# The normaliser of the decode states goes by transfer into and out of the states' 129th column

## The chip, the cores and the metric

The kernel runs on one core of a Trainium2 chip. The metric is the device time of one launch in microseconds (us); the figure compared is the median of several runs. A core has TensorE (matrix products; "PE" in the profile, "PEld" for its weight loads), VectorE ("DVE"), ScalarE ("ACT"), GpSimd ("POOL") and SyncE ("SP", which here issues all transfers). Each of them works through its own list of instructions in a fixed order, so an instruction that waits holds everything behind it in its list. Transfers run on 16 DMA engines.

## The reference

One decoder layer on 1024 prompt tokens and on 8 decode sequences of 8 tokens each. Half of the mixing heads are retention heads, half are mLSTM heads (4 of each, 128 wide). Cut to the mLSTM part that the change touches:

```python
def step(carry, inp):
    C, n, m = carry                       # matrix memory, normaliser, stabiliser
    ...
    num = (einsum('bhts,bhsv->bhtv', s, vc)
           + inter[..., None] * einsum('bhvd,bhtd->bhtv', C, qc))
    den_dot = sum(s, axis=-1) + inter * einsum('bhd,bhtd->bht', n, qc)
    ...
    C_new = decay[..., None, None] * C + einsum('bhsv,bhsd->bhvd', vc * wl[..., None], kc)
    n_new = decay[..., None] * n + einsum('bhs,bhsd->bhd', wl, kc)
```

`n` (128 numbers for each head and sequence) is treated like one more column of `C`: the same product with q and the same update. For the 8 decode sequences `C` and `n` come from the inputs and go back to the outputs.

## The kernel before, in words

The work is staged: input projections with the 8 heads between them, output projection, up-projection with a convolution, down-projection. `mix_head(hd, ml)` does one head, first the 4 retention heads, then the 4 mLSTM heads m0 to m3.

In one mLSTM head `proj` makes q, k and v, each from one 128x1024 weight tile that is fetched by `stage_w` (line 133, tile `st_in`, 2 buffers) and split by ScalarE (L145, `wh_in`) and VectorE (L147, `wl_in`) into a high and a low part for the matmuls of lines 159 to 161. Then `front` prepares two chunks of 128 tokens, `pair_of` does two chunks, `sample` does the 64 decode tokens, and `finish` normalises; the decode tokens stand third in `order = [[0, 1], [2, 3], [8], [4, 5], [6, 7]]`.

The decode states of a head lie in the tile `sb` of 128 partitions x 8 sequences x 129 columns: 128 columns for `C`, the 129th for `n`. There is one buffer for it (`bufs=1`), shared by all heads, so the next head's states can be written into it only when this head's are stored. Its steps: line 511 fetches `C` into the first 128 columns; lines 512 to 515 fetch `n` into a tile `sn` of its own and copy it on VectorE into the 129th column; line 617 multiplies `sb` with the queries on TensorE; lines 626 and 634 update it on VectorE; line 637 stores `C` (`out_cs`); lines 639 and 640 copy the 129th column back to `sn` and store that (`out_ns`).

Beside the mLSTM heads runs `weight_sums` (lines 692 to 707), which needs nothing from them: 40 times it fetches a 128x1024 group of up-projection weights into one of two tiles `sg` (lines 699 and 700, one buffer each), makes four differences on GpSimd (L704) and stores them to a DRAM scratch `sd` (L705). A fetch into a tile waits until the store before it has left that tile. All of these transfers and all others stand in the one list of SyncE.

The order in each list is not the order of the text: a scheduler puts the instructions in order at build time by its own estimate of the times, and inserts the waits on semaphores. What stands where is shown below with the change.

Of the kernel before, what the change touches and what calls it, by code (L numbers as in the profile page):

```python
# [10 lines left out]
F32 = mybir.dt.float32  # L11
# [5 lines left out]
P = 128  # L17
# [3 lines left out]
NB = 8  # L21
# [71 lines left out]
def hybrid_layer_kernel(ctx: ExitStack, tc: tile.TileContext, a: dict, o: dict):  # L93
    nc = tc.nc
# [32 lines left out]
    def bank(p, cols, name, rows=P, dt=F32):  # L127
        t = p.tile([P, 512], dt, tag="bank", name=name)
        return t[:rows, :cols]
# [95 lines left out]
    m2 = mpool("m2", bufs=2)  # L225
# [251 lines left out]
    def mix_head(hd, ml):  # L477

        nm = ("m" if ml else "r") + str(hd)
# [30 lines left out]
        sb = m2.tile([P, NB, 129], F32, tag="sb", bufs=1, name=f"sb_{nm}")  # L510
        nc.sync.dma_start(sb[:, :, :P], a["sc" if ml else "sr"][hd].rearrange("p (s v) -> p s v", s=NB))
        if ml:
            sn = m2.tile([P, NB], F32, tag="sn", name=f"sn_{nm}")
            nc.sync.dma_start(sn, a["sn"][hd])
            nc.vector.tensor_copy(sb[:, :, P], sn)
        dec = m2.tile([P, 16], F32, tag="dec", name=f"dec_{nm}")

        def front(cs):
# [52 lines left out]
        def stats(on, po, i0, L, n, mv, name):  # L571
            nc.scalar.activation(on[:n, i0:i0 + L, :W], po, AF.Copy)
            for i in range(i0, i0 + L):
                st = m2.tile([P, 6], F32, tag="bn", name=f"bn_{name}{i}")
                nc.vector.bn_stats(st[:n], on[:n, i, :P])
                nc.vector.bn_aggr(mv[:n, i, :], st[:n])

        def finish(on, mv, c0, L, name):

            n = rows_of(c0)  # L580
            sh = [n, L]
            small = lambda tag: m2.tile([P, 4], F32, tag=tag, name=f"{tag}_{name}")[:n, :L]
            vv, A = small("vv"), small("A")
            if ml:
                den, rd = small("den"), small("rd")
                dd = on[:n, :L, P]
                nc.vector.scalar_tensor_tensor(den, dd, -1.0, dd, ALU.mult, ALU.max)
                nc.vector.tensor_tensor(den, den, cols[:n, c0:c0 + L, hd], ALU.max)
                nc.vector.reciprocal(rd, den)
                nc.vector.tensor_tensor(vv, mv[:n, :L, 1], rd, ALU.mult)  # L590
                nc.vector.tensor_tensor(vv, vv, rd, ALU.mult)
            else:
                xs_ = lambda t: cst[:n, t + 9 * hd + c0:t + 9 * hd + c0 + L]
                rd = xs_(C_XI)
                nc.vector.tensor_tensor(vv, mv[:n, :L, 1], xs_(C_XI2), ALU.mult)
            nc.vector.tensor_scalar(vv, vv, EPS, None, ALU.add)
            rstd_small(A, vv, m2, name, sh)
            nc.vector.tensor_tensor(A, A, rd, ALU.mult)
            ps = bank(psB, L * n, f"yt_{name}")
            for i in range(L):  # L600
                nc.vector.tensor_scalar(on[:n, i, :P], on[:n, i, :P], mv[:n, i, 0:1], A[:, i:i + 1],
                                        ALU.subtract, ALU.mult)
                nc.tensor.transpose(ps[:, i * n:(i + 1) * n], on[:n, i, :P], ident[:n, :n])
            y = yT[hid // 2][:, hid % 2, c0 * CH:c0 * CH + L * n]
            gain = vec[:, V_HEAD + hid:V_HEAD + hid + 1]
            if hid in EARLY:
                nc.vector.scalar_tensor_tensor(y, ps, gain, y, ALU.mult, ALU.mult)
            else:
                nc.scalar.activation(y, ps, AF.Copy, scale=gain)

        def sample(kz, vt, qs, pt):
            qv = qs[:, 0, :TS] if ml else q[:, LP:]
            nc.vector.tensor_copy(qown, qv.rearrange("p (s l) -> p s l", s=NB))
            po = bank(psB, W, f"o_{nm}8", rows=TS)
            nc.tensor.matmul(po, pt[:TS, 0, :TS], vt[:TS, 0, :W], start=True, stop=False)
            for i in range(NB):
                nc.tensor.matmul(po, qx[:, i * TS:(i + 1) * TS], sb[:, i, :W], start=False, stop=i == NB - 1)
            on = m2.tile([P, 4, 129], F32, tag="on", bufs=3, name=f"on_{nm}s")
            mv = m2.tile([P, 4, 2], F32, tag="mv", bufs=3, name=f"mv_{nm}s")
            stats(on, po.unsqueeze(1), 0, 1, TS, mv, f"{nm}s")  # L620
            vx = m2.tile([TS, NB, 129], F32, tag="vx", bufs=1, name=f"vx_{nm}")[:, :, :W]
            e = nc.vector if ml else nc.gpsimd
            e.tensor_tensor(vx, vt[:TS, 0, :W].unsqueeze(1).broadcast_to([TS, NB, W]),  # L623
                            cst[:TS, C_BLK:C_BLK + NB].unsqueeze(2).broadcast_to([TS, NB, W]), ALU.mult)
            if ml:
                e.tensor_tensor(sb, sb, dec[:, 8:16].unsqueeze(2).broadcast_to([P, NB, W]), ALU.mult)
            step = 3 if ml else 4
            for j in range(0, NB, step):
                m = min(step, NB - j)
                up = bank(psB, m * W, f"us_{nm}{j}").rearrange("p (s v) -> p s v", s=m)  # L630
                nc.tensor.matmul(up, kz[:TS, 0, :], vx[:, j:j + m, :], start=True, stop=True)
                sj = sb[:, j:j + m, :W]
                if ml:
                    nc.vector.tensor_tensor(sj, sj, up, ALU.add)
                else:
                    nc.vector.scalar_tensor_tensor(sj, sj, math.exp(LS * LG[hd]), up, ALU.mult, ALU.add)
            nc.sync.dma_start(o["cs" if ml else "ss"][hd].rearrange("p (s v) -> p s v", s=NB), sb[:, :, :P])
            if ml:
                nc.vector.tensor_copy(sn, sb[:, :, P])
                nc.sync.dma_start(o["ns"][hd], sn)  # L640
            return lambda: finish(on, mv, 8, 1, f"{nm}s")

        S = None
# [35 lines left out]
        for i, cs in enumerate(order):  # L679
            cur, ready = ready, front(order[i + 1]) if i + 1 < len(order) else None  # L680
            done = sample(*cur) if cs == [8] else pair_of(cs[0], *cur)
            if todo:
                todo()
            todo = done
            next(rows, None)
# [24 lines left out]
    for hd in range(NH):  # L710
        mix_head(hd, False)
        if hd == 0:
            gate_proj()
            rows = gate_rows()
# [3 lines left out]
    for hd in range(NH):  # L718
        mix_head(hd, True)
# [610 lines left out]
```

## Time and profile before

| | us |
|---|---|
| median of 3 runs | 1426.72 |
| the runs | 1421.37 to 1428.78 |
| the profiled execution | 1421.1 |
| its span | 1419.3 |
| TensorE busy | 1350.3 (95%) |
| VectorE busy | 1005.3 (71%) |
| ScalarE busy | 587.7 (41%) |
| GpSimd busy | 386.3 (27%) |
| the 16 DMA engines busy, mean | 40% |

The span is the profiled execution on the core; the 1.8 us between it and the execution's own time lie around it. Times in rows of the profile count from the start of the span. A row of a timeline has the start, the duration, the engine, the line of the kernel, the operation and its tiles ("out<-in"), and in brackets the idle time before it and what ended that. "SPq" rows are instructions of SyncE that issue a transfer.

### The profile page before, as it was taken

To read this page: it belongs to the slowest core of one execution; us is meant where nothing else is said; L and a number is where in the kernel's file an instruction comes from. 1 tells how busy PE (TensorE), PEld (TensorE's weight loads), DVE (VectorE), ACT (ScalarE), POOL (GpSimd) and SP (SyncE) were. 2 spreads that over 40 slices of the span, in tenths; PEclk is the share of its full clock that TensorE was granted. 3 is DMA by queue.
4 is the path that set the end of the run, shared out by engine and by line. 5 is a ranking of instruction groups with operands and counts; after the bars stand their busy time and mean duration, and the time that the engine had idled before them with its cause. 6 is when DMAs were issued, how large, how long until landed. Compare 5 with 4: busy or idle time off the path is not lost.

```text
span 1419.3 us, 26935 instructions
## 1 busy us (share of the span) xinstructions
PE 1350.3 (95%) x10545; PEld 1324.8 (93%) x10545; DVE 1005.3 (71%) x2030; ACT 587.7 (41%) x1102; POOL 386.3 (27%) x486
## 2 busy tenths in 40 slices
PE   7999899999697799999999999999999999999996
PEld 7899899989687799999999999999999999999995
DVE  7846974464353546656889987877877889896677
ACT  6424543312131223544546444433443445454553
POOL 5200000244454450000244322122222115782000
PEclk9999999999899999999999999999999999999998
DMA  6112111455657652332314343344343358633363
GB/s 234 60 45 78 48 54 56 134 180 193 209 179 225 205 183 75 113 114 73 123 42 145 149 153 125 118 138 145 138 137 130 117 161 308 197 115 99 96 213 126
DMA packets 116286, 192.80 MB, mean 136 GB/s; under 512 B 9024, under 2 KB 74688, under 8 KB 115648
## 3 DMA queue, kind: packets, MB, share of 16 engines
q1 hardware_dynamic: 116160, 191.09, 40.1%
q8 instruction: 83, 1.36, 0.4%
q14 instruction: 43, 0.35, 0.1%
HBM read 134.58 MB, written 56.47 MB: 135 GB/s over the span
## 4 chain that ended last, share of the span: by engine, by line
PE 73%; DMA 13%; DVE 6%; POOL 3%; issue 2%; ACT 2%; SPq 1%; DVEq 0%; POOLq 0%; ACTq 0%
DMA sd<-sg 6%; PE up_S L958 6%; PE up_S L957 6%; PE up_S L956 6%; PE in L161 6%; PE in L159 5%; PE in L160 5%; DMA sg<-in_wu 5%; PE dn L1155 5%; PE dn L1153 5%; PE dn L1154 5%; PE up_A L957 4%; PE up_A L956 4%; PE up_A L958 4%; POOL sg L704 3%
## 5 line engine op out<-in xcount | busy, mean ns | idle before, releaser
L159 PE MATMUL in<-hh,wh_in 128*128 128x272 f32 x1024 | 304.9, 298 | 8.6 <-ACT hh L199 6.7
L161 PE MATMUL in<-hh,wl_in 128*128 128x272 f32 x1024 | 302.2, 296 | 1.4 <-DVE wl_in L147 1.4
L160 PE MATMUL in<-hl,wh_in 128*128 128x272 f32 x1024 | 301.0, 294 | 1.3 <-DVE hl L200 1.3
L159 PEld LDWEIGHTS in<-hh,wh_in 128*128 128x128 f32 x1024 | 196.9, 192 | 10.7 <-ACT hh L199 6.6
L160 PEld LDWEIGHTS in<-hl,wh_in 128*128 128x128 f32 x1024 | 196.3, 192 | 3.8 <-issue 2.1
L161 PEld LDWEIGHTS in<-hh,wl_in 128*128 128x128 f32 x1024 | 196.2, 192 | 3.0 <-DVE wl_in L147 1.9
L704 POOL TENSOR_TENSOR sg<-sg 128x256 f32<-128x256 f32 x160 | 124.4, 790 | 175.5 <-DMA sg<-in_wu 167.8
L145 ACT ACTIVATE wh_up<-st_up 128x1024 fp32r<-128x1024 f32 x84 | 80.5, 959 | 165.4 <-PE up_S L957 99.6
L1082 DVE TENSOR_TENSOR rb<-rb 128x544 fp32r<-128x544 f32 x78 | 76.5, 986 | 37.8 <-ACT rb L1081 37.6
L147 DVE TENSOR_TENSOR wl_up<-st_up,wh_up 128x1024 fp32r<-128x1024 f32 x84 | 95.9, 1142 | 7.9 <-ACT wh_up L145 7.8
L930 DVE TENSOR_TENSOR Uv<-Uv,up_S 128x272 f32<-128x272 f32 (+1 forms) x200 | 66.7, 377 | 46.0 <-PE up_S L958 46.0
L986 POOL TENSOR_TENSOR act<-act 128x544 f32<-128x544 f32 x44 | 70.6, 1604 | 78.3 <-DMA bd<-act 50.0
L1081 ACT ACTIVATE rb<-rb 128x544 fp32r<-128x544 f32 x78 | 50.5, 650 | 75.4 <-DMA rb<-bd 62.8
L1102 POOL TENSOR_TENSOR wd<-wd 128x512 f32<-128x512 f32 x44 | 73.7, 1701 | 27.8 <-DMA wd<-in_wd 15.0
L971 DVE SCALAR_TENSOR_TENSOR c<-Uv,vec,c 128x1024 f32<-128x1024 f32 (+1 forms) x88 | 70.1, 799 | 8.9 <-ACT c L969 8.9
L971 DVE SCALAR_TENSOR_TENSOR c<-Ug,vec,c 128x1024 f32<-128x1024 f32 x88 | 68.6, 819 | 1.3 <-ACT c L969 1.3
L145 ACT ACTIVATE wh_in<-st_in 128x1024 fp32r<-128x1024 f32 x32 | 33.9, 1058 | 54.5 <-PE in L160 48.6
L969 ACT ACTIVATE c<-Ug,vec 128x1024 f32<-128x1024 f32 (+1 forms) x44 | 34.6, 835 | 52.2 <-DVE Ug L934 47.0
L921 POOL MEMSET Ug<- 128x2 f32 x22 | 2.2, 99 | 177.4 <-DVE xr L824 83.7
L147 DVE TENSOR_TENSOR wl_in<-st_in,wh_in 128x1024 fp32r<-128x1024 f32 x32 | 41.1, 1283 | 10.9 <-ACT wh_in L145 10.4
L623 POOL TENSOR_TENSOR vx_r<-vts,cst 64x1024 f32<-64x1024 f32 x4 | 8.3, 2082 | 142.7 <-ACT vts L536 142.7
L958 PE MATMUL up_S<-T1h,wl_up 128*128 128x272 f32 x160 | 46.6, 291 | 0.0
(540 smaller groups left out, 4583.3 us busy)
## 6 DMA issues: line engine op xcount, KB each, us to landing
rb<-bd SPq DMA_DIRECT2D x76, 272.0 KB, 2.9
sg<-in_wu SPq DMA_DIRECT2D x80, 256.0 KB, 3.9
sd<-sg SPq DMA_DIRECT2D x40, 512.0 KB, 4.0
st_up<-sd SPq DMA_DIRECT2D x40, 512.0 KB, 3.7
bd<-act SPq DMA_DIRECT2D x33, 544.0 KB, 4.5
st_in<-in_wi SPq DMA_DIRECT2D x32, 512.0 KB, 4.3
st_up<-in_wu SPq DMA_DIRECT2D x24, 512.0 KB, 4.1
wd<-in_wd SPq DMA_DIRECT2D x44, 256.0 KB, 4.6
```

What stands on the lines that cost most here:

```text
L145: nc.scalar.activation(hi, x, AF.Copy)
L147: eng.tensor_tensor(lo, x, hi.bitcast(F32), ALU.subtract)
L159: nc.tensor.matmul(ps, hi[:, ws], xh, start=k == 0, stop=False)
L160: nc.tensor.matmul(ps, hi[:, ws], xl, start=False, stop=False)
L161: nc.tensor.matmul(ps, lo[:, ws], xh, start=False, stop=k == KT - 1)
L704: nc.gpsimd.tensor_tensor(o_, x, y, op)
L956: nc.tensor.matmul(ps, wh[:, c], xh[:, k, n], start=k == 0, stop=False)
L957: nc.tensor.matmul(ps, wh[:, c], xl[:, k, n], start=False, stop=False)
L958: nc.tensor.matmul(ps, wl[:, c], xh[:, k, n], start=False, stop=k == 3)
L971: nc.vector.scalar_tensor_tensor(c, u(i), cw(i), c, ALU.mult, ALU.add)
L1082: nc.vector.tensor_tensor(lo, x, hi.bitcast(F32), ALU.subtract)
L1102: nc.gpsimd.tensor_tensor(quad(p, out), quad(p, x), quad(p, y), op)
```

## The change

The tile `sn` and its two copies on VectorE go. `n` is fetched by a transfer straight into the 129th column of `sb`, and stored straight from there. `C` and its two transfers stay.

```diff
         sb = m2.tile([P, NB, 129], F32, tag="sb", bufs=1, name=f"sb_{nm}")
         nc.sync.dma_start(sb[:, :, :P], a["sc" if ml else "sr"][hd].rearrange("p (s v) -> p s v", s=NB))
         if ml:
-            sn = m2.tile([P, NB], F32, tag="sn", name=f"sn_{nm}")
-            nc.sync.dma_start(sn, a["sn"][hd])
-            nc.vector.tensor_copy(sb[:, :, P], sn)
+            nc.sync.dma_start(sb[:, :, P], a["sn"][hd])
...
             nc.sync.dma_start(o["cs" if ml else "ss"][hd].rearrange("p (s v) -> p s v", s=NB), sb[:, :, :P])
             if ml:
-                nc.vector.tensor_copy(sn, sb[:, :, P])
-                nc.sync.dma_start(o["ns"][hd], sn)
+                nc.sync.dma_start(o["ns"][hd], sb[:, :, P])
```

The 8 numbers of `n` in a partition lie 129 columns apart in `sb`, so each of the two transfers now moves 1024 pieces of 4 bytes, where it moved 128 pieces of 32 bytes.

The lists of ScalarE and GpSimd keep their order. On VectorE the 8 copies are left out, and in each mLSTM head the decode tokens' last normalising step (`on_m0s`) changes places with the step after it (`kz_m`); TensorE takes three transposes and one matmul in another order there. Two places matter below.

On VectorE, at the end of head m0 (names with `m0s` are its decode tokens), before the change, the copy into the next head's `sb` stands between two small steps of m0's normalising:

```order
L591 TENSOR_TENSOR vv_m0s<-vv_m0s,rd_m0s 64x1
L596 TENSOR_SCALAR vv_m0s<-vv_m0s 64x1
L171 SCALAR_TENSOR_TENSOR t_m0s<-t_m0s,vv_m0s 64x1
L515 COPY sb_m_4493<-sn_m_4495 128x8
L172 SCALAR_TENSOR_TENSOR A_m0s<-t_m0s,r_m0s 64x1
L598 TENSOR_TENSOR A_m0s<-A_m0s,rd_m0s 64x1
L601 TENSOR_SCALAR on_m0s<-on_m0s,mv_m0s,A_m0s 64x128
```

The same place after the change (lines below the edit are numbered 2 or 3 lower):

```order
L589 TENSOR_TENSOR vv_m0s<-vv_m0s,rd_m0s 64x1
L594 TENSOR_SCALAR vv_m0s<-vv_m0s 64x1
L171 SCALAR_TENSOR_TENSOR t_m0s<-t_m0s,vv_m0s 64x1
L172 SCALAR_TENSOR_TENSOR A_m0s<-t_m0s,r_m0s 64x1
L596 TENSOR_TENSOR A_m0s<-A_m0s,rd_m0s 64x1
L526 TENSOR_TENSOR kz_m_4012<-x_m_4007,cols 128x256
L599 TENSOR_SCALAR on_m0s<-on_m0s,mv_m0s,A_m0s 64x128
```

What waited for the buffer `sb` here (the copy) is gone, and nothing in this part of VectorE's list touches `sb` any more.

On SyncE, where m0's states are stored and m1's are fetched, before the change (`sn_m_5226` is already that of m2; those of m0 and m1 are fetched near the start of the kernel):

```order
L637 DMA out_cs<-sb_m_3762 1024x1x128
L640 DMA out_ns<-sn_m_3764 128x8
L699 DMA sg_1_4733<-in_wu 128x2x256
L700 DMA sg_1_4733<-in_wu 128x2x256
L511 DMA sb_m_4493<-in_sc 128x8x128
L514 DMA sn_m_5226<-in_sn 128x8
L705 DMA sd<-sg_0_4725 512x1x256
```

After the change:

```order
L635 DMA out_cs<-sb_m_3762 1024x1x128
L637 DMA out_ns<-sb_m_3762 1024x1x1
L696 DMA sg_1_4727<-in_wu 128x2x256
L697 DMA sg_1_4727<-in_wu 128x2x256
L511 DMA sb_m_4490<-in_sc 128x8x128
L513 DMA sb_m_4490<-in_sn 128x8x1
L702 DMA sd<-sg_0_4719 512x1x256
```

The places are the same; the fetch into `sb` now waits for both stores out of it, and every head's `n` is fetched right behind its `C`. So in heads m0 and m3 one transfer more than before stands here, and in m1 and m2 the place of `sn` is taken over; the two fetches of `n` near the start of the list are gone.

## Prediction

> **What bounds the kernel now.** I read the chain of work that ended last first, on the page and then in order of time. On the page it is mostly TensorE, but transfers and GpSimd's weight sums are in it:
>
> ```profile
> PE 73%; DMA 13%; DVE 6%; POOL 3%; issue 2%; ACT 2%; SPq 1%; DVEq 0%; POOLq 0%; ACTq 0%
> ```
>
> In order of time that part is one stretch (start, length, what):
>
> ```profile
> 264.27 4.58 DMA sg<-in_wu
> ...
> 489.62 3.46 DMA out_ns<-sn_m
> 496.65 0.86 PE u_m L656 x4
> ```
>
> From 264 to 489 us, during the mLSTM heads, the chain is nothing but weight sums: fetch, difference, store, next fetch. They don't need the heads. At 489.6 the chain passes through a store of states and comes back to TensorE. So something of the heads waited for SyncE's list. The waits of VectorE and of TensorE between 255 and 560 us say what (who <- for whom: us in total, times, longest):
>
> ```profile
> DVE sb_m L515 <- DMA out_cs<-sb_m: 24.2, 2, 14.2
> DVE sb_m L515 <- DMA out_ns<-sn_m: 11.5, 1, 11.5
> DVE sb_m L515 <- DMA out_ss<-sb_r: 5.0, 1, 5.0
> PE yt_m0s L603 <- DVE on_m0s L601: 12.4, 1, 12.4
> PE o_m L661 <- DVE pt_m L568: 8.5, 1, 8.5
> PE yt_m2s L603 <- DVE on_m2s L601: 7.8, 1, 7.8
> PE cols L400 <- DVE cols L401: 2.5, 1, 2.5
> ```
>
> The copy L515 stands on VectorE for 40.7 us in four waits, until the last head's states have left `sb`; their stores stand in SyncE's list behind weight sums. Behind each L515 waits what TensorE needs next, and TensorE idles four times, 31.2 us in all. The view has no other wait of it in this stage. After each pause its granted clock is about half for some 3.5 us (window, length, busy of PE, PEld, DVE, ACT and POOL, granted clock, DMA share, GB/s):
>
> ```profile
> 299.30:302.60 3.30, 3.29 (x15) 3.10 (x16) 1.59 (x9) 0.80 (x1) 3.14 (x6) 0.53 0.74 228
> 367.80:371.50 3.70, 3.68 (x18) 3.58 (x18) 3.39 (x9) 1.77 (x4) 3.08 (x4) 0.54 0.88 272
> 433.20:437.00 3.80, 3.80 (x21) 3.80 (x21) 3.06 (x10) 0.39 (x1) 3.63 (x4) 0.63 0.84 266
> 494.20:498.00 3.80, 3.79 (x19) 3.68 (x20) 3.37 (x9) 1.77 (x4) 2.40 (x3) 0.57 0.93 272
> ```
>
> A pause so costs its length and (1 - clock) of these windows: 2.5 + 1.6, 12.4 + 1.7, 8.5 + 1.4, 7.8 + 1.6, thus 4.1, 14.1, 9.9 and 9.4 us for m0 to m3. All four together are 37.5 us, the most that the change can bring here.
>
> **What becomes late next.** It can't bring all of that, because the weight tiles of the projections stand in the same SyncE list, and the list goes at the pace of the weight sums. `st_in` is fetched two tiles ahead. Counting fetches (L133) and splits (L145) off against each other from the first on, the three fetches below (issues) belong to the three splits under them, each at the end of a head's v projection:
>
> ```profile
> 375.45 0.72 SPq L133 DMA_DIRECT2D st_in<-in_wi  x1
> 440.10 0.45 SPq L133 DMA_DIRECT2D st_in<-in_wi  x1
> 499.98 0.63 SPq L133 DMA_DIRECT2D st_in<-in_wi  x1
> ```
>
> ```profile
> 395.93 1.06 ACT L145 ACTIVATE wh_in<-st_in 128x1024 fp32r<-128x1024 f32 x1 [2.48 <-PE in L160]
> 459.49 1.06 ACT L145 ACTIVATE wh_in<-st_in 128x1024 fp32r<-128x1024 f32 x1 [2.48 <-DMA sg<-in_wu]
> 522.27 1.06 ACT L145 ACTIVATE wh_in<-st_in 128x1024 fp32r<-128x1024 f32 x1 [2.48 <-PE in L160]
> ```
>
> Until a fetch has landed, ScalarE stands at its L145, and behind it stand the exponentials and scaled copies of `front`, on which TensorE depends after about 2.3 us of projection matmuls:
>
> ```profile
> 461.95 0.37 PE L159 MATMUL in<-hh,wh_in 128*128 128x272 f32 x1
> 464.30 0.61 PE L656 MATMUL u_m<-vts,kz_m 128*128 128x129 f32 x4
> ```
>
> A fetch lands about 4.3 us after its issue (the median, "st_in<-in_wi"):
>
> ```profile
> st_in<-in_wi SPq DMA_DIRECT2D x32, 512.0 KB, 4.3
> ```
>
> So TensorE can run ahead of the old schedule by at most 395.93 - 375.45 - 4.3 + 2.3 = 18.5 us in m1, 459.49 - 440.10 - 4.3 + 2.3 = 17.4 us in m2 and 522.27 - 499.98 - 4.3 + 2.3 = 20.3 us in m3. I call these the three gates. They move later by as much as the change delays SyncE's list.
>
> **The price of the transfers in 4-byte pieces.** The trace of before has none, only the same number of pieces at 512 bytes, and 32-byte pieces. Both were alone on the rings at m3's stores (two windows of the DMA view, 541.9:551 and 544:551; the second holds the end of the first):
>
> ```profile
> DMA packets 1184, 0.53 MB, mean 58 GB/s; under 512 B 160, under 2 KB 1184, under 8 KB 1184
> q1 hardware_dynamic: 1184, 0.53, 21.2%
> DMA packets 291, 0.07 MB, mean 10 GB/s; under 512 B 160, under 2 KB 291, under 8 KB 291
> q1 hardware_dynamic: 291, 0.07, 4.5%
> ```
>
> 21.2% of 16 engines for 9.1 us are 30.9 us, 4.5% of 16 for 7 us are 5.0 us. The 893 large pieces between them took 25.8 us, 28.9 ns each; the 160 small ones (128 of `out_ns` and 32 still smaller) then (5040 - 131 x 28.9) / 160 = 7.8 ns each. A transfer of 1024 pieces puts 64 on each engine: 0.5 us at the small price, 1.85 us at the large one. Before, 8 pieces took 0.06 us. I take 0.5 us, since 4 bytes are nearest to the 32-byte pieces, and keep 1.8 us as the other end.
>
> The Trainium skill speaks against this edit: its page "DMA: Bandwidth & Descriptors", in Rules for kernel authors, says that a strided last dimension becomes one descriptor per element and should be rearranged to be contiguous, and under Specifications that below 512 B a transfer reads, changes and writes back. The trace agrees that small pieces cost a fixed amount each, and its 32-byte pieces show no writing back in their 7.8 ns; by the page alone each transfer would be nearer the large price or above it. What that gives is the third rival.
>
> SyncE itself: an issue of 1024 pieces (L511) takes 0.54 us, those of `n` now 0.47 and 0.66 us, so the issues keep their price (min/median/max ns, then first and last start):
>
> ```profile
> L511 SPq DMA_DIRECT2D sb_m<-in_sc x4: 539/539/592, 298.6 to 493.1; - x4
> L514 SPq DMA_DIRECT2D sn_m<-in_sn x4: 328/465/656, 19.2 to 432.2; - x4
> L640 SPq DMA_DIRECT2D out_ns<-sn_m x4: 617/659/820, 361.9 to 541.8; - x4
> ```
>
> Where they stand in m0 and m2:
>
> ```profile
> 298.59 0.54 SPq L511 DMA_DIRECT2D sb_m<-in_sc  x1
> 300.32 0.56 SPq L705 DMA_DIRECT2D sd<-sg  x1
> ...
> 488.97 0.60 SPq L637 DMA_DIRECT2D out_cs<-sb_m  x1
> 489.62 0.66 SPq L640 DMA_DIRECT2D out_ns<-sn_m  x1
> ```
>
> In m0 the added L513 (the new fetch of `n`) falls between L511 and the next store, where the list stood still for 1.2 us, so it costs nothing there; if that cover is gone, some 0.6 us; in m3, where a fetch is also added, 0.6 us at most. The fetch of `C` now waits for both stores; `out_ns` is issued 0.65 us behind `out_cs`, so the fetch and what is behind it move by up to 0.7 us in m1 to m3. I take 0.4 us for each of these heads, as part of it falls into waits like m0's. Fewer small fetches near the start (two of L514) may give back up to 2 x 0.66 us or nothing; I take nothing, because TensorE starts there on other tiles.
>
> **The sum.** Before gate 1 stand three of the new transfers, before gate 2 five, before gate 3 seven. At 0.5 us each plus 0.4 us for each head whose fetch waits for the second store, the gates come 1.9, 3.3 and 4.7 us later. TensorE is ahead by 4.1 us after m0 and 18.2 after m1. Gate 1 allows 18.5 - 1.9 = 16.6, a pause of 1.6 us, too short to cost clock (the 2.5 us pause is the shortest that did). Then 16.6 + 9.9 = 26.5; gate 2 allows 17.4 - 3.3 = 14.1, a pause of 12.4 us, and half clock after it takes 1.6 us more: 12.5. Then 12.5 + 9.4 = 21.9; gate 3 allows 20.3 - 4.7 = 15.6, and with the clock 14.0.
>
> The last fetch of `st_in` and its split were:
>
> ```profile
> 533.00 0.62 SPq L133 DMA_DIRECT2D st_in<-in_wi  x1
> 563.22 1.06 ACT L145 ACTIVATE wh_in<-st_in 128x1024 fp32r<-128x1024 f32 x1 [0.76 <-PE in L160]
> ```
>
> Between them 563.22 - 533.00 - 4.3 = 25.9 us are left, so this one doesn't bind, and the later stages move along as a whole. At the large price gate 3 comes 7 x 1.8 + 1.2 = 13.8 us later: 20.3 - 13.8 - 1.6 = 4.9 us are left. With transfers and clock at nothing it is 20.3.
>
> VectorE's eight copies go; those of L515 take 0.23 us (median), L639's move the same 128x8. Beside busy TensorE they count nothing; if that cover were gone, they would be worth 8 x 0.23 = 1.9 us:
>
> ```profile
> L515 DVE COPY sb_m<-sn_m x4: 174/234/745, 298.6 to 493.1; 128x8 f32<-128x8 f32 x4
> L617 PE MATMUL o_m<-sb_m,qx x64: 271/273/324, 342.6 to 538.0; 128*64 128x129 f32 x64
> ```
>
> L617, which needs the fetched states, starts 44 us after L515 in m0 and in m3 (first and last starts of the two rows). With TensorE 22 us ahead and a landing after some 5 us more than 15 us are left, so the wait doesn't simply move there.
>
> The profiled execution took 1421.1 us; 14.0 less is 1407. It is one of the faster ones: the median is 1426.7, and the same difference from that gives 1413 us, my forecast. About 0.5% (7 us) is what a measurement of this kernel can tell from no change; the runs before lie within 7.4 us of each other.
>
> **The rivals.** First, the gates don't hold: TensorE finds other work while ScalarE waits, and all 37.5 us come through, 1389 us. For it speaks that TensorE waited for nothing else in this stage; against it that SyncE's list, not the heads, is the chain from 264 to 489 us, and that one list serves both. Chance 0.08.
>
> Second, no change: the 4-byte pieces cost about as much as the 512-byte ones and all of it lies on the weight sums' chain. That leaves the 4.9 us worked out, 1422 us. For it speaks that this chain has no slack, against it the 7.8 ns. Chance 0.20.
>
> Third, slower: a 4-byte piece costs more than a 512-byte one, for example twice (57.8 ns) if it is read and written back. Then a transfer holds the rings for 3.7 us, gate 3 comes 7 x 3.7 + 1.2 = 27.1 us later, and 20.3 - 27.1 - 1.6 = -8.4: 1435 us. The sign turns where a transfer takes (20.3 - 1.6 - 1.2) / 7 = 2.5 us, 39 ns a piece; nothing that small took so long in this trace. By the page's sentence on reading and writing back this is the case to expect. Chance 0.10.
>
> The forecast, a gain between 7 and 20 us held by gate 3, has the remaining 0.62. Faster by over 0.5% is it and the first rival, 0.70; the same 0.20; slower 0.10. The range takes gate 3 without any cost (a gain of 20.3: 1406) and a little beyond towards the first rival, and reaches past the second rival to the small end of the third: 1403 to 1425 us. What is left out is most of 0.08 and of 0.10.
>
> **What would show it.** Right: no row of VectorE waiting for `out_cs` or `out_ns`; TensorE's four waits of 12.4, 8.5, 7.8 and 2.5 us gone; new ones in their place in m2 and m3, about 12 and 6 us, behind `vts` or `wt` of ScalarE, with ScalarE's L145 waiting for `st_in`; the fetch now at 499.98 us issued 3 to 8 us later; small packets below 10 ns. Wrong: transfers of `n` that take 3 us or more on the rings, a pause of TensorE at L617 for the states, or a mLSTM stage without any pause.

## The result, and the profile after

The changed kernel takes 1430.88 us, median of 20 runs (1425.34 to 1435.92); the kernel before, in 20 runs, 1422.96 us. The ratio is 1.005, 95% interval 1.0036 to 1.0064: slower by 7.9 us, where 1413 us (14 less than before) was forecast. The profiled execution has a span of 1430.4 us, 11.1 more than before.

In the chain of work that ended last, on the profile's page after, DMA's share falls from 13% to 9%, and GpSimd's from 3% to 1%, yet the time is longer: a share of the chain doesn't say what a stage costs. In order of time (start, length, what) one finds the states' store and the weight tile's fetch in it:

```profile
362.25 12.99 DMA sg<-in_wu
...
438.23 11.60 DMA out_ns<-sb_m
...
460.04 4.74 DMA st_in<-in_wi
...
509.59 14.79 DMA sd<-sg
```

Before, a link of weight sums there was 3 to 6 us long. Here the two that run beside the states' stores take 13 and 15 us.

The waits of TensorE between 255 and 590 us (who <- for whom: total, times, longest), and those of ScalarE:

```profile
PE u_m L653 <- ACT vts L534: 41.2, 3, 18.9
```

```profile
ACT wh_in L145 <- DMA st_in<-in_wi: 56.2, 3, 23.9
```

The copy L515 and TensorE's four pauses behind it are gone. Three others are there, 41.2 us instead of 31.2, behind `vts`, which ScalarE makes after its L145; these are the three gates. The difference of 10.0 us is nearly the whole 11.1 us of the span. The timeline of SyncE shows why the gates are late. First at m0's end, then the first fetch behind it and the fetches of gates 2 and 3:

```profile
360.88 0.61 SPq L635 DMA_DIRECT2D out_cs<-sb_m  x1
361.53 0.68 SPq L637 DMA_DIRECT2D out_ns<-sb_m  x1
...
364.36 0.61 SPq L697 DMA_DIRECT2D sg<-in_wu  x1
373.88 0.54 SPq L511 DMA_DIRECT2D sb_m<-in_sc  x1
...
384.24 1.07 SPq L133 DMA_DIRECT2D st_in<-in_wi  x1
...
460.04 0.48 SPq L133 DMA_DIRECT2D st_in<-in_wi  x1
...
528.35 0.63 SPq L133 DMA_DIRECT2D st_in<-in_wi  x1
```

SyncE's list stands from 365 to 373.9 us until both stores have left `sb`. The gates' fetches are issued at 384.24, 460.04 and 528.35 us, 8.8, 19.9 and 28.4 us later than before: 8.8, 11.1 and 8.5 us for each of the three stores that lie ahead of them. Issues and their median time to landing (DMA view, 255 to 560 us; KB each, us), after and before:

```profile
out_cs<-sb_m SPq DMA_DIRECT2D x4, 512.0 KB, 11.1
...
sb_m<-in_sn SPq DMA_DIRECT2D x4, 4.0 KB, 5.3
...
out_ns<-sb_m SPq DMA_DIRECT2D x4, 4.0 KB, 13.0
```

```profile
out_cs<-sb_m SPq DMA_DIRECT2D x4, 512.0 KB, 4.1
...
out_ns<-sn_m SPq DMA_DIRECT2D x4, 4.0 KB, 4.2
sn_m<-in_sn SPq DMA_DIRECT2D x2, 4.0 KB, 4.4
```

The fetch of `n` in 4-byte pieces lands 0.9 us later than the old one; the store lands 8.8 us later, and the store of `C` beside it, which nobody changed, 7.0 us later. A window behind m0's stores (length, busy of the engines, granted clock, DMA share, GB/s), after and before:

```profile
362.00:376.00 14.00, 14.00 (x114) 14.00 (x113) 2.11 (x3) 2.89 (x5) 2.92 (x4) 1.00 0.69 92
```

```profile
362.00:376.00 14.00, 8.18 (x54) 8.10 (x55) 6.78 (x21) 2.55 (x6) 6.59 (x8) 0.67 0.71 221
```

The DMA engines count as busy as before (0.69 against 0.71), but move 92 GB/s instead of 221. Behind m1's stores, from 441 to 449 us, it is 0.88 against 0.70, with 73 instead of 243 GB/s.

### The profile page after: what moved, and what is told of

It reads as the page before. It is cut to its first block, busy times and chain, and to the rows that moved or that the text cites. A ratio compares the mean times of both kernels' runs of the same rounds, so it can differ in the third digit from the quotient of the medians.

```text
span 1430.4 us, 26927 instructions
## 1 busy us (share of the span) xinstructions
PE 1351.8 (95%) x10545; PEld 1325.6 (93%) x10545; DVE 1007.9 (70%) x2022; ACT 587.4 (41%) x1102; POOL 388.1 (27%) x486
## 4 chain that ended last, share of the span: by engine, by line
PE 76%; DMA 9%; DVE 8%; issue 3%; ACT 2%; SPq 1%; POOL 1%; DVEq 0%; ACTq 0%; POOLq 0%
PE in L161 7%; PE in L160 7%; PE in L159 7%; PE up_S L955 5%; PE up_S L954 5%; PE up_S L953 5%; PE up_A L954 4%; PE up_A L953 4%; PE up_A L955 4%; PE dn L1152 4%; PE dn L1150 4%; PE dn L1151 4%; DMA sd<-sg 3%; DMA sg<-in_wu 2%; PE out L161 1%
## 5 line engine op out<-in xcount | busy, mean ns | idle before, releaser
L159 PEld LDWEIGHTS in<-hh,wh_in 128*128 128x128 f32 x1024 | 195.9, 191 | 10.9 <-ACT hh L199 6.7
L145 ACT ACTIVATE wh_up<-st_up 128x1024 fp32r<-128x1024 f32 x84 | 80.5, 958 | 164.4 <-PE up_S L954 99.4
L145 ACT ACTIVATE wh_in<-st_in 128x1024 fp32r<-128x1024 f32 x32 | 33.9, 1058 | 102.2 <-DMA st_in<-in_wi 59.4
L653 PE MATMUL u_m<-vts,kz_m 128*128 128x129 f32 x64 | 12.2, 319 | 41.2 <-ACT vts L534 41.2
L653 PEld LDWEIGHTS u_m<-vts,kz_m 128*128 128x128 f32 x64 | 9.9, 220 | 42.2 <-ACT vts L534 41.8
```

Source lines behind the costliest of these rows:

```text
L145: nc.scalar.activation(hi, x, AF.Copy)
L159: nc.tensor.matmul(ps, hi[:, ws], xh, start=k == 0, stop=False)
```

## The experiments

All ratios are to the kernel before, measured on the same chip; three chips were used, so versions are compared by their ratios. The first four tell apart fetch from store, and the store's piece size from its place in DRAM.

**Only the fetch changed.** Against the changed kernel, the store goes by the old copy again:

```diff
-                nc.sync.dma_start(o["ns"][hd], sb[:, :, P])
+                sn = m2.tile([P, NB], F32, tag="sn", name=f"sn_{nm}")
+                nc.vector.tensor_copy(sn, sb[:, :, P])
+                nc.sync.dma_start(o["ns"][hd], sn)
```

> Only the fetch of n goes straight into the 129th column; the store goes through sn and a copy on VectorE, as before the change. Theory S (the stores in 4-byte pieces into DRAM hold the rings some 9 us each, the fetches cost next to nothing): the wait of VectorE for the buffer is gone, the gates come only 2 to 3 us later than in the kernel before, gate 3 leaves a gain of 20.3 - 2.5 - 1.6 = 16 us: ratio 0.989 (0.985 to 0.992). Theory F (the fetches in 4-byte pieces carry a good part of the loss): gate 3 over 10 us later, ratio 0.995 or more.

Measured: 1400.77 us, ratio 0.9875 (0.9848 to 0.9903). TensorE's only wait of note in this stage, and the landings:

```profile
PE u_m L655 <- ACT vts L534: 13.2, 2, 10.9
```

```profile
out_cs<-sb_m SPq DMA_DIRECT2D x4, 512.0 KB, 4.8
...
sb_m<-in_sn SPq DMA_DIRECT2D x4, 4.0 KB, 5.1
...
out_ns<-sn_m SPq DMA_DIRECT2D x4, 4.0 KB, 3.9
```

The fetch in 4-byte pieces costs next to nothing, and this version beats both kernels. What is left behind the gates is a pause of 10.9 us in m2 and one of 2.3 us in m3.

**Only the store changed.** The old fetch with its copy, the new store:

```diff
-            nc.sync.dma_start(sb[:, :, P], a["sn"][hd])
+            sn = m2.tile([P, NB], F32, tag="sn", name=f"sn_{nm}")
+            nc.sync.dma_start(sn, a["sn"][hd])
+            nc.vector.tensor_copy(sb[:, :, P], sn)
```

> Only the store of n goes straight from the 129th column; the fetch goes through sn and a copy on VectorE, as before the change. Theory S: L515 now waits for both stores; it comes as much later as the fetch of the states did in the changed kernel, near 28 us at m3, and TensorE with it: about 1450 us, ratio 1.019 (1.013 to 1.025). Theory F: the loss was in the fetches, so about as before, ratio 1.000 to 1.004.

Measured: 1450.76 us, ratio 1.0232 (1.0209 to 1.0256). The copy now waits for the slow store itself (waits of VectorE):

```profile
DVE sb_m L515 <- DMA out_ns<-sb_m: 70.3, 3, 24.3
```

The whole loss lies in the store. The new fetch without the copy hides part of it in the changed kernel: it is worth some 26 us beside the slow store (1.0232 against 1.005) and 17 us without it. That is near the 17 to 20 us by which the gates let TensorE run ahead, but no run shows that this is why.

**No small pieces at all.** `n` lies beside `C` in the input and output arrays in DRAM, and one transfer of 128 rows of 4128 bytes goes each way:

```diff
-        nc.sync.dma_start(sb[:, :, :P], a["sc" if ml else "sr"][hd].rearrange("p (s v) -> p s v", s=NB))
-        if ml:
-            nc.sync.dma_start(sb[:, :, P], a["sn"][hd])
+        nc.sync.dma_start(sb[:, :, :W], a["sc" if ml else "sr"][hd].rearrange("p (s v) -> p s v", s=NB))
...
-            nc.sync.dma_start(o["cs" if ml else "ss"][hd].rearrange("p (s v) -> p s v", s=NB), sb[:, :, :P])
-            if ml:
-                nc.sync.dma_start(o["ns"][hd], sb[:, :, P])
+            nc.sync.dma_start(o["cs" if ml else "ss"][hd].rearrange("p (s v) -> p s v", s=NB), sb[:, :, :W])
```

> n lies beside C in DRAM, so that one transfer with 128 pieces of 4128 bytes fetches all 129 columns and one stores them; no copies, no sn. Theory S: no small piece is left, the wait on VectorE is gone, and the gates of the prediction hold: gain 17 to 20 us, ratio 0.987 (0.984 to 0.990). If the gates are no gates: a gain of 37 us, ratio 0.974. If what is lost in the changed kernel comes from the order of the lists and not from the pieces: 1.000 or more.

Measured: 1402.39 us, ratio 0.9885 (0.9864 to 0.9906). What is left of pauses:

```profile
PE u_m L649 <- ACT vts L532: 10.5, 2, 5.3
```

Without any transfer of `n` the gain is that of the version with the changed fetch, within both intervals: 16 and 17 us. Both have no pause of note left but those behind `vts`, which points to the gates.

**The stored numbers apart in DRAM.** As the changed kernel, but each number of the output `n` has 64 bytes, in a second version 512 bytes, of DRAM to itself:

```diff
-                nc.sync.dma_start(o["ns"][hd], sb[:, :, P])
+                nc.sync.dma_start(o["ns"][hd][:, :, 0], sb[:, :, P])
...
-    "ns": (NH, P, NB), "m": (NH, 16), "conv": (P, 2 * JT * 18),
+    "ns": (NH, P, NB, 16), "m": (NH, 16), "conv": (P, 2 * JT * 18),
```

> As the changed kernel, but each 4-byte number of the stored n has 64 bytes of DRAM to itself; the same 1024 pieces. Theory L (4-byte writes into the same short stretch of DRAM hold each other up): the store gets cheap, landing about 4 to 5 us, ratio 0.990. Theory P (each 4-byte write into DRAM is slow wherever it goes): landing stays at 11 us or more, ratio 1.003 to 1.010.

Measured at 64 bytes: 1409.95 us, ratio 0.9935 (0.9914 to 0.9957).

```profile
out_cs<-sb_m SPq DMA_DIRECT2D x4, 512.0 KB, 6.1
sb_m<-in_sn SPq DMA_DIRECT2D x4, 4.0 KB, 4.3
out_ns<-sb_m SPq DMA_DIRECT2D x4, 4.0 KB, 6.1
```

The same 1024 pieces of 4 bytes from the same tile, and the store lands after 6.1 us instead of 13.0. So neither the number nor the size of the pieces makes the loss by itself, but 4-byte writes close together in DRAM. Some 0.6% is left against the version with the changed fetch; hence the second version:

> As the kernel with the stored numbers 64 bytes apart in DRAM (0.9935, stores landed after 6.1 us), but 512 bytes apart. If the 4-byte writes still hold each other up at 64 bytes, the stores now land after 4 to 5 us and the ratio comes to 0.988 (0.985 to 0.991), that of the kernel with only the fetch changed. If what is left at 64 bytes is a price of each write into DRAM alone, landing (about 6 us) and ratio stay: 0.9935 (0.991 to 0.996).

Measured at 512 bytes: 1408.9 us, ratio 0.9902 (0.9877 to 0.9927).

```profile
out_ns<-sb_m SPq DMA_DIRECT2D x4, 4.0 KB, 5.4
```

The landing falls a little further, to a value between the two expectations, and the ratio is at the upper end of the first range; but the intervals of the two versions overlap. Whether the rest is a price of each write or still nearness isn't settled.

**The pieces read from the tile without writing them to DRAM.** The 129th column is copied into `sn` by a transfer, and `sn` stored as before the change:

```diff
-                nc.sync.dma_start(o["ns"][hd], sb[:, :, P])
+                sn = m2.tile([P, NB], F32, tag="sn", name=f"sn_{nm}")
+                nc.sync.dma_start(sn, sb[:, :, P])
+                nc.sync.dma_start(o["ns"][hd], sn)
```

> As the changed kernel, but n is stored in two steps: a transfer copies the 4-byte pieces out of the 129th column into a tile of 128x8 in the on-chip memory, and from there goes the old store of 32-byte pieces. Theory W (writing 4-byte pieces into neighbouring places of DRAM is what is slow): the copy lands after about 5 us like the fetch of n, the store after about 4 us; C of the next head waits some 1 us longer than in the kernel with only the fetch changed (0.9875), so a ratio of 0.990 (0.986 to 0.994). Theory R (reading 4-byte pieces 516 bytes apart from the on-chip memory is slow): the copy lands after 10 us or more, and the ratio is 1.002 or above, as in the changed kernel.

Measured: 1408.05 us, ratio 0.9888 (0.9865 to 0.9911).

```profile
sn_m<-sb_m SPq DMA_DIRECT2D x4, 4.0 KB, 4.6
out_ns<-sn_m SPq DMA_DIRECT2D x4, 4.0 KB, 2.4
```

Theory W holds: reading 4-byte pieces out of the tile costs nothing of note, even in front of a second transfer.

**The slow store without a waiter.** The version with the changed fetch, each list in the same order, but the copy of `n` has gaps, so that its store is 4-byte pieces again, from a tile for which `C`'s fetch doesn't wait:

```diff
-                sn = m2.tile([P, NB], F32, tag="sn", name=f"sn_{nm}")
-                nc.vector.tensor_copy(sn, sb[:, :, P])
-                nc.sync.dma_start(o["ns"][hd], sn)
+                sn = m2.tile([P, NB, 2], F32, tag="sn", name=f"sn_{nm}")
+                nc.vector.tensor_copy(sn[:, :, 0], sb[:, :, P])
+                nc.sync.dma_start(o["ns"][hd], sn[:, :, 0])
```

> The kernel with only the fetch changed (0.9875), every list in the same order, but the tile that holds the copy of n for the store has a gap of 4 bytes behind each number, so that its store is 1024 pieces of 4 bytes again. Nothing but the same head's next use of that tile waits for this store: C's fetch waits for the store of C alone. Theory Q (what costs is that the next head's C, and SyncE's list behind it, wait for the slow store to land): the gain stays, 0.989 (0.986 to 0.992), with C stored after about 5 us and SyncE held no longer than there. Theory B (what costs is that the slow store holds the rings, so that the store of C and the weight sums' fetches beside it are late too): C lands after about 11 us as in the changed kernel, the weight fetches come 15 us or more late in m3, and the ratio is 1.000 or above.

Measured: 1433.38 us, ratio 1.0098 (1.0081 to 1.0114). The gain of the version with the changed fetch is gone and more, though only the pieces of one small store differ. TensorE's waits and the landings:

```profile
PE u_m L655 <- ACT vts L534: 42.1, 3, 20.7
```

```profile
out_cs<-sb_m SPq DMA_DIRECT2D x4, 512.0 KB, 10.6
...
out_ns<-sn_m SPq DMA_DIRECT2D x3, 4.0 KB, 14.4
```

The same 14 us behind m0's stores in this version, and in that with the changed fetch:

```profile
362.00:376.00 14.00, 14.00 (x114) 14.00 (x114) 1.89 (x3) 2.89 (x5) 2.90 (x4) 1.00 0.79 69
```

```profile
362.00:376.00 14.00, 14.00 (x114) 14.00 (x113) 1.67 (x2) 2.89 (x5) 6.85 (x8) 1.00 0.76 220
```

Theory B holds. Until the store has landed, the transfers beside it are late, at the same busy share (0.79 and 0.76) with 69 instead of 220 GB/s. That is (220 - 69) GB/s x 14 us = 2.1 MB less, or 9.6 us at 220 GB/s, near the 8.5 to 11.1 us by which each store delayed the gates in the changed kernel. No instruction waits for the small store in this version, so that wait is not what costs.

**The gates' fetches taken out of SyncE's list.** In two versions ScalarE issues the 16 fetches of projection weights that concern the mLSTM heads, from the version without small pieces and from the changed kernel:

```diff
-        nc.sync.dma_start(st, src)
+        (nc.scalar if name in {f"in{i}" for i in range(16, 32)} else nc.sync).dma_start(st, src)
```

> The kernel with n beside C in DRAM (0.9885; TensorE pauses of 5.2 us in two heads behind ScalarE's wait for weight tiles), and the 16 fetches of projection weights from the last retention head to m3 issued by ScalarE itself, behind its own splits, so that SyncE's list no longer sets when they start. Theory G (three gates: these fetches in SyncE's list hold back the rest of the 37.5 us): the two pauses go, 10.5 us and about 3 us of half clock less, ratio 0.979 (0.975 to 0.982). Rival (something else is late next, the states' fetch or the rings): a new pause of about the same length elsewhere, ratio 0.985 or above.

> The changed kernel (slow 4-byte stores left in), with the same 16 fetches of projection weights issued by ScalarE instead of SyncE. Theory Q (the slow stores cost their time through SyncE's list: the list stands while C waits for them, and the weight fetches behind it come late): the three pauses of 9.9, 18.9 and 12.4 us behind ScalarE's scaled copies fall to a few us in all, and what remains is the states' own fetch in m3, which lands only some 4 us before the matmul that needs it: ratio 0.993 (0.987 to 0.998). Theory B (the slow stores hold up all transfers on the rings wherever they are issued): the weight fetches land after 8 us or more, the pauses stay, ratio 1.001 or above.

Measured: 1423.64 us, ratio 1.0003 (0.9988 to 1.0019), and 1447.86 us, ratio 1.0163 (1.0141 to 1.0186). Both came out worse than their twins. In the second the weight fetches land after 4.4 us, and the pauses behind `vts` are nearly gone, but TensorE waits longer elsewhere. ScalarE's timeline at m0's end shows what for:

```profile
379.64 0.34 ACTq L133 DMA_DIRECT2D st_in<-in_wi  x1
380.02 0.39 ACT L570 ACTIVATE on_m<-o_m 128x258 f32<-128x258 f32 x1 [22.58 <-DMA sg<-in_wu]
```

ScalarE stands 22.58 us at its own issue of a fetch, until a weight sum's fetch has landed. In the list as built this issue carries two waits, one for the buffer and one on a completion counter (DMAHW4) that transfers of SyncE use too:

```
L133 DMA st_in22_4998<-in_wi 128x1024 [waits DMAHW4_49,DVE_49]
```

So the fetches seem to have taken the coupling to the weight sums along, and now hold ScalarE's list. The first version went the way of theory G's rival, but its new pauses are longer, some 25 us in all instead of 10.5. The second came out above theory Q's range, and its weight fetches land too early for theory B as worded there, because all but one are issued when no slow store is running. That one fits theory B. It is issued at 447.46 us, 4.3 us behind m1's small store, by ScalarE on a queue of its own (q10). From 447.4 to 456 us SyncE's queue (q1) is the only one with packets; the first of q10 starts 8.6 us after the issue, some 3 us after the store has landed, where the other 15 start within 2.5 us. The DMA view from 447.4 to 456 us, and of q10 from 456 to 459 us (packets, MB, share of 16 engines):

```profile
q1 hardware_dynamic: 554, 0.54, 49.6%
```

```profile
q10 hardware_dynamic: 144, 0.52, 42.7%
```

Neither run tells whether the gates alone hold back the rest of the 37.5 us. That the counter is the cause fits the rows but wasn't tried by itself.

## Why the prediction was wrong

- **What bounds the kernel, right.** VectorE's wait for `out_cs` and `out_ns` and TensorE's four pauses are gone, and no wait for the states at the matmul of the fetched states took their place.
- **The three gates, right.** The new pauses are where the prediction put them, and the version with only the fetch changed gains 17.4 us (1418.19 to 1400.77 us) of the possible 37.5. The forecast of 14.0 was even low for it: the gates did not come later by 1.9 to 4.7 us there; their three fetches of `st_in` are issued 1.0 to 2.8 us earlier than the 375.45, 440.10 and 499.98 us of before:

```profile
372.65 1.03 SPq L133 DMA_DIRECT2D st_in<-in_wi  x1
...
439.11 0.45 SPq L133 DMA_DIRECT2D st_in<-in_wi  x1
...
497.84 0.74 SPq L133 DMA_DIRECT2D st_in<-in_wi  x1
```

- **The price of the transfers in 4-byte pieces, wrong; this is the step that failed.** The prediction took the pieces' own time, 64 on each engine at 7.8 ns, for the time that the transfer holds the rings, and gave this one price, 0.5 us with 1.85 us as the large end, to fetches and stores. The fetch fits it. The store took some 9 us of the rings: gate 3 came 28.4 us later, not 4.7. Yet the pieces' own time was right. The DMA view, 441 to 449 us of the changed kernel:

```profile
DMA packets 1894, 0.58 MB, mean 73 GB/s; under 512 B 1065, under 2 KB 1893, under 8 KB 1893
...
q1 hardware_dynamic: 1893, 0.57, 87.2%
```

  87.2% of 16 engines for 8 us are 111.6 us. The trace keeps the size and time of each packet: the 1065 small ones took 9.0 ns each (9.6 us), 544 of 512 bytes 27 ns each (14.7 us), and 284 of 1024 bytes, those of the weight sums, 307 ns each (87.3 us). Between 366 and 371 us, behind m0's store, there is no small packet at all, and 97 larger ones fill 60.0% of 16 engines for 5 us, 495 ns each. In the version with only the fetch changed, packets of the same kind (372 to 374 us, 642 in 31.0 us) took 48 ns each. The two views:

```profile
DMA packets 97, 0.10 MB, mean 20 GB/s; under 512 B 0, under 2 KB 97, under 8 KB 97
...
q1 hardware_dynamic: 97, 0.10, 60.0%
```

```profile
q1 hardware_dynamic: 642, 0.64, 96.9%
```

  So the sign "small packets below 10 ns" came true in a kernel that got slower: the cost lies on the transfers behind the pieces until the store has landed, and the pieces' own time doesn't hold it. "4 bytes are nearest to the 32-byte pieces" chose the row by size; neither window that gave the two prices held a store into DRAM in pieces of less than 32 bytes, so they were no bounds.
- **The third rival, right in its place and sign, by other transfers.** With gate 3 at 28.4 us its formula gives 20.3 - 28.4 - 1.6 = -9.7 us, against 11.1 in the span and 7.9 between the medians. It had 3.7 us for each of seven transfers, from 57.8 ns for each piece; it was some 9 us for each of three stores, at 9.0 ns for each piece. That 26 us and 28 us come out so close is luck. A chance of 0.10 was too low for a price that no row bounded and against which the Trainium skill spoke.
- **The page's sentence.** The Trainium skill, "DMA: Bandwidth & Descriptors", Specifications, says that below 512 B a transfer reads, changes and writes back. The direction was right for the store. But the fetch of as many 4-byte pieces, their copy between tiles, and their store at 64 bytes' distance landed after 5.1, 4.6 and 6.1 us, so it is no fixed price for each small piece here. Whether the close writes hold each other up by such writing back wasn't shown.

## What to carry to other kernels

A copy on an engine that gathers scattered numbers before a store is worth keeping when it turns 4-byte writes to neighbouring addresses into longer ones; the way in, scattering by a fetch, can do without it. Price fetch and store apart, and where the trace has no row for a kind of write, measure it or leave its upper bound open. When a small transfer is suspect, compare the GB/s of a window at equal DMA share: its harm shows in its neighbours, while its own packets looked as cheap as ever (9.0 ns).

## What the runs showed of the hardware

A store of 1024 pieces of 4 bytes into one stretch of 4 KB of DRAM landed after 13.0 us (median), held the transfers beside it to a third of the bytes (69 instead of 220 GB/s over 14 us, with all lists equal), and looks like busy DMA engines in the profile. Its own packets took 9.0 ns each; it was the packets of 1024 bytes behind them that took 307 ns (441 to 449 us of the changed kernel) and 495 ns (366 to 371 us) instead of 48. A fetch on another queue, issued 4.3 us behind such a store, had its first packet 8.6 us later. With the pieces 64 bytes apart it landed after 6.1 us, at 512 bytes after 5.4 us. The same pieces fetched from DRAM landed after 5.1 us, copied between tiles after 4.6 us; 128 pieces of 32 bytes stored took 4.2 us.
